# Hybrid decoder layer on one core: the stacked MLP operand as one contiguous piece, wide matmuls in groups, and a rewritten opening unit

## The chip, the core and the metric

The kernel runs on one core of a Trainium2 chip. A core has five engines with queues of their own: TensorE (PE: matmuls and transposes; PEld is its weight load), VectorE (DVE), ScalarE (ACT), GpSimd (POOL) and SyncE (SP, which here only issues transfers). They work in parallel and meet at semaphores. Matmuls write PSUM, which has eight banks of 128 partitions x 512 fp32 values; ACT and DVE read it and write SBUF. The metric is device microseconds of one execution, lower is better.

## The reference, cut to what matters

One decoder layer, 256 positions, width 2048, all fp32. `h = RMSNorm(x)` goes through a wide projection into a gated DeltaNet branch (A), an HGRN2 branch (B), a cross-attention into 256 memory tokens (C) and gates; the branches are merged, projected and added to `x`; then an MLP of width 8192 follows. The two pieces that the change touches are the memory's keys and values, and the MLP:

```
mem_n = rmsnorm(mem, g_mem)                   # (256, 2048)
kv = mem_n @ w_kv                             # (2048 -> 2048): k | v
...
x  = x + rmsnorm(merged @ w_out, g_post_mix)
h2 = rmsnorm(x, g_pre_mlp)
m  = square(relu(h2 @ w_mlp_in)) @ w_mlp_out  # 2048 -> 8192 -> 2048
x  = x + rmsnorm(m, g_post_mlp)
```

## The kernel before, in words

**Precision.** Every large product is formed from split operands: `hi` is the value rounded to the matmul type fp32r, `lo` is the rest. `a @ w` is `hi*hi + hi*lo + lo*hi`, three matmuls into one PSUM accumulation. Weights arrive as fp32 tiles `w` of 2 k-tiles x 512 columns (512 KB, one transfer on SP's queue, four buffers). ACT casts them to `wh` (L145), and DVE subtracts to get `wl` (L147).

**Units.** A unit is 512 output columns over all k-tiles. Kind "x" (L182 to L184) holds 128 positions stationary and streams 512 weight columns; kind "w" (L189 to L191) holds 128 weight columns stationary and streams 256 positions. In both, three matmuls follow each other per product. The third form is `unit_stacked` (L207, L208), used for 15 of the 16 units of the MLP's first matrix. Stationary are 128 weight columns; a first, wide matmul streams `hi` and `lo` of the activations together (2 x 256 columns) against `wh`, then a narrow one streams `hi` (256 columns) against `wl`. The four 128-column blocks `c` of a weight tile go to four banks. The activations stand in tiles `h2h` made by `h8`, laid out `[hi/lo, k-tile, 256]`, so that `hi` and `lo` of one k-tile lie four k-tiles apart and the wide matmul's moving operand has two pieces.

**The MLP.** It runs in eight steps of 1024 hidden columns: `mlp_in(e)` is two units (32 k-tile visits, 128 wide-narrow pairs), then `mlp_out(e-1)` is four kind "x" units of 8 k-tiles (192 matmuls). `mlp_in` evicts each of the four banks with an ACT copy and a DVE add (L1112 and the line after).

**The opening.** Nothing can be multiplied before memory, gain and weights are there. Unit 0 (values of the memory, kind "x") fetches `mem` in `load_mem` between its weight loads, turns it on TensorE (`tr`, L232), and evicts the transposes with the gain as a column scale: `split_scaled` has ACT write `memh` (L216) and DVE write `meml` (L217), k-tile by k-tile. Two k-tiles share one PSUM bank. The program's framework does not let two engines touch a bank at once: the ACT eviction of the second k-tile waits for the DVE eviction of the first. The order of instructions on each engine is chosen by a scheduler, except those that are pinned in program order (`keep_in_program_order`, here `pin`). The squares of `mem` (L325) for the norm run after unit 0, as the first step of `gen_start`, a generator whose steps are pumped one per weight group; it also loads `x` and the small vectors.

**The turn from mixer to MLP.** `mix_last(ps, t)` finishes the residual for 128 positions: a square, a reciprocal root on POOL, four updates of `x` on DVE, and for each of four column chunks `c` four transposes into one bank and four `split_scaled` calls into `h2h`.

Of the kernel before, what the change touches and what calls it, by code (L numbers as in the profile page):

```python
# [33 lines left out]
KG = 2  # L34
BL = 16
WB = 4
NPIN = 1
# [4 lines left out]
def tile_trunk(ctx: ExitStack, tc, a):  # L42
# [23 lines left out]
    def h8(name):  # L66

        return hp.tile([P, 2, 4, S], F32R, tag="h", name=nm(name))
# [24 lines left out]
    pinned = [NPIN]  # L93
# [6 lines left out]
    def load_gcol(names, c0, q):  # L100
        n = len(names) * 16
        grow = const(f"grow{c0}", [n, P])
        for i, x_ in enumerate(names):
            q(grow[i * 16:(i + 1) * 16, :], a[x_][0].rearrange("(c p) -> c p", p=P))
        pg = bank("gcol")
        T.transpose(pg[:, 0:n], grow, ident[0:n, 0:n])
        V.tensor_copy(gcol[:, c0:c0 + n], pg[:, 0:n])

    load_gcol(["g_mem"], 0, adma)
# [28 lines left out]
    def load_w(src, k0, n, c0, width=512, home=None):  # L138
        w = wp.tile([P, KG, 512], F32, tag="w", name=nm("w"), bufs=WB)
        nc.sync.dma_start(  # L140
            w[:, 0:n, 0:width],
            src[k0 * P:(k0 + n) * P, c0:c0 + width].rearrange("(k p) n -> p k n", p=P),
        )
        wh = home("wh") if home else wp.tile([P, KG, 512], F32R, tag="wh", name=nm("wh"))
        i_hi = A.copy(wh[:, 0:n, 0:width], w[:, 0:n, 0:width])  # L145
        wl = home("wl") if home else wp.tile([P, KG, 512], F32R, tag="wl", name=nm("wl"))
        i_lo = V.tensor_tensor(out=wl[:, 0:n, 0:width], in0=w[:, 0:n, 0:width],  # L147
                               in1=wh.bitcast(F32)[:, 0:n, 0:width], op=ALU.subtract)
        if pinned[0] > 0:
            pinned[0] -= 1  # L150
            pin(i_hi)
            pin(i_lo)
        return wh, wl

    def unit(kind, act, nk, src, c0, r0=0, pre=None, order=None, split=False, post=None, ws=None):
# [12 lines left out]
        for i, (g, tt) in enumerate(order):  # L168
            k0 = g * KG
            if pre is not None:  # L170
                pre(k0)
# [25 lines left out]
    def unit_stacked(pairs, nk, src, c0, ps):  # L197


        for g in range(nk // KG):  # L200
            k0 = g * KG
            wh, wl = load_w(src, k0, KG, c0)
            for j in range(KG):
                kt = k0 + j
                both = pairs[kt // 4][:, :, kt % 4, :]
                for c in range(4):
                    T.matmul(ps[c], wh[:, j, c * P:(c + 1) * P], both, start=kt == 0, stop=False)  # L207
                    T.matmul(ps[c][:, 0:S], wl[:, j, c * P:(c + 1) * P], both[:, 0, :], start=False, stop=kt == nk - 1)  # L208
# [5 lines left out]
    def split_scaled(ps, hi, lo, col):  # L214

        A.activation(hi, ps, AF.Copy, scale=col)  # L216
        V.scalar_tensor_tensor(out=lo, in0=ps, scalar=col, in1=hi.bitcast(F32),  # L217
                               op0=ALU.mult, op1=ALU.subtract)
# [5 lines left out]
    def transpose_chunk(src, tiles, c, col0, halves=(0, 1)):  # L224

        hi, lo = tiles
        for half in halves:
# [6 lines left out]
            for q in range(2):  # L234
                kk = half * 2 + q
# [21 lines left out]
    def load_mem(k0):  # L257
# [6 lines left out]
        for sl in cols:  # L264
            nc.sync.dma_start(t[:, :, sl], mem_r[:, :, c * 512 + sl.start:c * 512 + sl.stop])
# [921 lines left out]
```

## Time and profile before

| | |
|---|---|
| median of 3 runs (lowest to highest) | 1843.23 us (1843.05 to 1844.44) |
| profiled execution, its own time | 1843.67 us |
| span of its instructions | 1841.9 us, so 1.8 us lie around it |
| PE busy in the span | 1819.5 us (99%) |
| DVE, ACT busy | 1111.0 us (60%), 900.3 us (49%) |
| first slice of 46 us: PE busy | 7 tenths |

A matmul's busy time in this profile is modelled and runs into the next one: a 512-column matmul reads 0.39 us, while the next starts 0.227 us later. What one really costs is read from the distance between starts, or from the number of matmuls in a stretch. A view by windows lists for each stretch the busy time of each engine with its number of instructions in brackets, then the granted TensorE clock, the mean busy share of the DMA engines and GB/s.

### The profile page before, as it was taken

To read this page: it belongs to the slowest core of one execution; us is meant where nothing else is said; L and a number is where in the kernel's file an instruction comes from. 1 tells how busy PE (TensorE), PEld (TensorE's weight loads), DVE (VectorE), ACT (ScalarE), POOL (GpSimd) and SP (SyncE) were. 2 spreads that over 40 slices of the span, in tenths; PEclk is the share of its full clock that TensorE was granted. 3 is DMA by queue.
4 is the path that set the end of the run, shared out by engine and by line. 5 is a ranking of instruction groups with operands and counts; after the bars stand their busy time and mean duration, and the time that the engine had idled before them with its cause. 6 is when DMAs were issued, how large, how long until landed. Compare 5 with 4: busy or idle time off the path is not lost.

```text
span 1841.9 us, 25658 instructions
## 1 busy us (share of the span) xinstructions
PE 1819.5 (99%) x10214; PEld 1586.4 (86%) x10214; DVE 1111.0 (60%) x1414; ACT 900.3 (49%) x1126; POOL 39.9 (2%) x68
## 2 busy tenths in 40 slices
PE   7999999999999999999999999999999999999997
PEld 5999999988899898888888888888888888888886
DVE  4755576764763685875455557655556565656556
ACT  5644565544545565644444445544444444444443
POOL 1000000200100000000000000000000000000000
PEclk9999999999999999999999999999999999999999
DMA  6766556664584555555766675666666666666663
GB/s 207 234 173 181 152 149 177 176 187 125 169 211 133 153 170 150 158 163 171 217 185 188 196 231 170 186 193 191 189 192 188 190 215 186 194 185 194 186 192 136
DMA packets 174649, 333.52 MB, mean 181 GB/s; under 512 B 13096, under 2 KB 14272, under 8 KB 174272
## 3 DMA queue, kind: packets, MB, share of 16 engines
q1 hardware_dynamic: 168976, 325.10, 58.6%
q10 hardware_dynamic: 4528, 4.54, 0.9%
q0 software_dynamic: 1024, 2.23, 0.7%
q8 instruction: 80, 1.31, 0.3%
q14 instruction: 41, 0.34, 0.1%
HBM read 329.60 MB, written 2.23 MB: 180 GB/s over the span
## 4 chain that ended last, share of the span: by engine, by line
PE 97%; DVE 1%; DMA 0%; issue 0%; ACT 0%; SPq 0%; POOL 0%; DVEq 0%; POOLq 0%; ACTq 0%
PE mm L182 18%; PE mm L184 18%; PE mm L183 18%; PE mm L207 12%; PE mm L208 6%; PE mm L189 6%; PE mm L191 6%; PE mm L190 6%; PE pa L917 1%; PE pw L745 1%; PE pzt L750 1%; DMA mem<-in_mem 0%; DVE wl L147 0%; PE tr L232 0%; PE ab L532 0%
## 5 line engine op out<-in xcount | busy, mean ns | idle before, releaser
L147 DVE TENSOR_TENSOR wl<-w,wh 128x1024 fp32r<-128x1024 f32 x608 | 741.1, 1223 | 596.8 <-ACT wh L145 595.6
L145 ACT CAST wh<-w 128x1024 fp32r<-128x1024 f32 x608 | 637.3, 1051 | 809.8 <-PE mm L184 470.4
L207 PE MATMUL mm<-h2h,wh 128*128 128x512 f32 x960 | 338.6, 398 | 0.0
L208 PE MATMUL mm<-h2h,wl 128*128 128x256 f32 x960 | 269.0, 280 | 0.0
L182 PE MATMUL mm<-wh,hh 128*128 128x512 f32 x576 | 228.4, 397 | 0.0
L184 PE MATMUL mm<-wh,hh 128*128 128x512 f32 x576 | 224.9, 391 | 0.0
L183 PE MATMUL mm<-wl,hh 128*128 128x512 f32 x576 | 224.3, 389 | 0.0
L189 PE MATMUL mm<-hh,wh 128*128 128x256 f32 x768 | 218.8, 285 | 0.0
L207 PEld LDWEIGHTS mm<-h2h,wh 128*128 128x128 f32 x960 | 180.3, 188 | 44.3
L191 PE MATMUL mm<-hh,wl 128*128 128x256 f32 x768 | 217.4, 283 | 0.1
L190 PE MATMUL mm<-hh,wh 128*128 128x256 f32 x768 | 217.3, 283 | 0.0
L182 PE MATMUL mm<-wh,mh 128*128 128x512 f32 x512 | 199.4, 389 | 0.0
L184 PE MATMUL mm<-wh,ml 128*128 128x512 f32 x512 | 199.3, 389 | 0.0
L183 PE MATMUL mm<-wl,mh 128*128 128x512 f32 x512 | 199.2, 389 | 0.0
L208 PEld LDWEIGHTS mm<-h2h,wl 128*128 128x128 f32 x960 | 181.2, 189 | 0.3
L189 PEld LDWEIGHTS mm<-hh,wh 128*128 128x128 f32 x768 | 147.3, 192 | 0.2
L191 PEld LDWEIGHTS mm<-hh,wl 128*128 128x128 f32 x768 | 147.2, 192 | 0.3 <-DVE wl L147 0.3
L190 PEld LDWEIGHTS mm<-hh,wh 128*128 128x128 f32 x768 | 147.3, 192 | 0.2
L184 PEld LDWEIGHTS mm<-wh,hh 128*128 128x128 f32 x576 | 108.1, 188 | 23.1
L183 PEld LDWEIGHTS mm<-wl,hh 128*128 128x128 f32 x576 | 108.4, 188 | 20.9
L182 PEld LDWEIGHTS mm<-wh,hh 128*128 128x128 f32 x576 | 108.3, 188 | 20.6
L184 PEld LDWEIGHTS mm<-wh,ml 128*128 128x128 f32 x512 | 96.1, 188 | 20.2
(361 smaller groups left out, 2167.0 us busy)
## 6 DMA issues: line engine op xcount, KB each, us to landing
w<-in_w_in SPq DMA_DIRECT2D x240, 512.0 KB, 3.7
w<-in_w_mlp_in SPq DMA_DIRECT2D x128, 512.0 KB, 3.7
w<-in_w_mlp_out SPq DMA_DIRECT2D x128, 512.0 KB, 3.7
w<-in_w_kv_mem SPq DMA_DIRECT2D x32, 512.0 KB, 5.3
w<-in_w_out SPq DMA_DIRECT2D x32, 512.0 KB, 4.3
w<-in_w_br_c SPq DMA_DIRECT2D x16, 512.0 KB, 4.2
w<-in_w_br_a SPq DMA_DIRECT2D x16, 512.0 KB, 3.9
w<-in_w_br_b SPq DMA_DIRECT2D x16, 512.0 KB, 3.7
```

The source lines that it names most:

```text
L145: i_hi = A.copy(wh[:, 0:n, 0:width], w[:, 0:n, 0:width])
L147: i_lo = V.tensor_tensor(out=wl[:, 0:n, 0:width], in0=w[:, 0:n, 0:width], in1=wh.bitcast(F32)[:, 0:n, 0:width], op=ALU.subtract)
L182: T.matmul(o, st, wh[:, j, :], start=kt == 0, stop=False)
L183: T.matmul(o, st, wl[:, j, :], start=False, stop=False)
L184: T.matmul(o, sl, wh[:, j, :], start=False, stop=kt == nk - 1)
L189: T.matmul(o, sh, ah, start=kt == 0 and c % 2 == 0, stop=False)
L190: T.matmul(o, sh, al, start=False, stop=False)
L191: T.matmul(o, sl, ah, start=False, stop=kt == nk - 1 and c % 2 == 1)
L207: T.matmul(ps[c], wh[:, j, c * P:(c + 1) * P], both, start=kt == 0, stop=False)
L208: T.matmul(ps[c][:, 0:S], wl[:, j, c * P:(c + 1) * P], both[:, 0, :], start=False, stop=kt == nk - 1)
L745: T.matmul(pw[:, b * 64:(b + 1) * 64], U[:, b, :], half_view(X, s, False)[:, b], start=True, stop=True)
L750: T.matmul(pzt[:, b * 64:(b + 1) * 64], W[:, b, :], half_view(XT, s, True)[:, b], start=True, stop=True)
```

## The change

The tiles of `h8` become `[k-tile, hi/lo, 256]`, so `hi` and `lo` of a k-tile are adjacent and the wide matmul's moving operand is one run of 512 columns. `unit_stacked` issues the four wide matmuls of a k-tile, then the four narrow ones. `split_scaled` takes a list and emits all ACT evictions, then all DVE ones. Unit 0 gets a function of its own, `first_unit`: its loads are pinned on SP, its transposes and products on PE, and the evictions and casts of the first two groups on ACT and DVE; the first weight tile comes in two pieces; each k-tile's transposes have a bank of their own; 19 transposes of the identity whose result nobody reads are added around the first real ones; `mem` squares are taken between groups; and `gen_start` issues its small loads at other steps.

```
 def h8(name):
-    return hp.tile([P, 2, 4, S], F32R, tag="h", name=nm(name))
+    return hp.tile([P, 4, 2, S], F32R, tag="h", name=nm(name))
...
 def unit_stacked(pairs, nk, src, c0, ps):
...
-    both = pairs[kt // 4][:, :, kt % 4, :]
+    both = pairs[kt // 4][:, kt % 4].rearrange("p s n -> p (s n)")
     for c in range(4):
         T.matmul(ps[c], wh[:, j, c * P:(c + 1) * P], both, start=kt == 0, stop=False)
-        T.matmul(ps[c][:, 0:S], wl[:, j, c * P:(c + 1) * P], both[:, 0, :], start=False, stop=kt == nk - 1)
+    for c in range(4):
+        T.matmul(ps[c][:, 0:S], wl[:, j, c * P:(c + 1) * P], both[:, 0:S], start=False, stop=kt == nk - 1)
...
-def split_scaled(ps, hi, lo, col):
-    A.activation(hi, ps, AF.Copy, scale=col)
-    V.scalar_tensor_tensor(out=lo, in0=ps, scalar=col, in1=hi.bitcast(F32),
-                           op0=ALU.mult, op1=ALU.subtract)
+def split_scaled(parts, q=lambda i: i):
+    for ps, hi, lo, col in parts:
+        q(A.activation(hi, ps, AF.Copy, scale=col))
+    for ps, hi, lo, col in parts:
+        q(V.scalar_tensor_tensor(out=lo, in0=ps, scalar=col, in1=hi.bitcast(F32),
+                                 op0=ALU.mult, op1=ALU.subtract))
...
+def load_mem(g):
+    c, half = g // 2, g % 2
...
+    if c < 2:
+        sl = slice(half * 256, half * 256 + 256)
+    elif half == 0:
+        sl = slice(0, 512)
+    else:
+        return
+    pin(nc.sync.dma_start(mem_s[c][:, :, sl], mem_r[:, :, c * 512 + sl.start:c * 512 + sl.stop]))
+
+def idle_turns(n):
+    pd = bank("idle")
+    for i in range(n):
+        pin(T.transpose(pd[:, i % 4 * P:(i % 4 + 1) * P], ident, ident))
+
+def first_unit(src, c0):
...
+    def fetch(g):
+        load_mem(g)
+        ws[g] = load_w_raw(src, g * KG, KG, c0, step=1 if g == 0 else None, q=pin)
+    def turn(g):
+        hi, lo = memT[g // 2]
+        parts = []
+        for kt in (g * KG, g * KG + 1):
+            pt, kk = bank("tr"), kt % 4
+            for t in range(NT):
+                pin(T.transpose(pt[:, t * P:(t + 1) * P], mem_s[g // 2][:, t, kk * P:(kk + 1) * P], ident))
+            parts.append((pt[:, 0:S], hi[:, kk, :], lo[:, kk, :], gcol[:, kt:kt + 1]))
+        split_scaled(parts, pin if g < 2 else lambda i: i)
...
+    fetch(0)
+    idle_turns(11)
+    turn_grow(grow_mem, 16, 0, pin)
+    turn(0)
+    idle_turns(8)
+    for g in range(ng):
+        wh, wl = split_w(ws.pop(g), KG, step=1 if g == 0 else None, q=pin if g < 2 else lambda i: i)
+        if g + 1 < ng:
+            fetch(g + 1)
+        products(g * KG, wh, wl)
+        if g + 1 < ng:
+            turn(g + 1)
+        products(g * KG + 1, wh, wl)
+        if g % 2 == 0 and g > 0:
+            sumsq_chunk(mem_s[g // 2 - 1], ssm, g // 2 - 1)
+        tick()
+    sumsq_chunk(mem_s[3], ssm, 3)
...
-            for k in range(4):
-                split_scaled(pt[:, k * P:(k + 1) * P], h2T[c][0][:, k, t * P:(t + 1) * P],
-                             h2T[c][1][:, k, t * P:(t + 1) * P], gcol[:, 32 + c * 4 + k:33 + c * 4 + k])
+            split_scaled([(pt[:, k * P:(k + 1) * P], h2T[c][0][:, k, t * P:(t + 1) * P],
+                           h2T[c][1][:, k, t * P:(t + 1) * P], gcol[:, 32 + c * 4 + k:33 + c * 4 + k]) for k in range(4)])
```

**The order on ACT in the opening.** Each row is an instruction in the order of the engine: line, operation, what is written from what, shape. `memh` from `tr` is the eviction of one k-tile of the turned memory, `wh` from `w` a weight cast (each number is another tile), `junk` a square of `mem`. Before, from the first eviction on:

```order
L216 ACTIVATE memh_128<-tr_131,gcol 128x256
L216 ACTIVATE memh_128<-tr_159,gcol 128x256
L216 ACTIVATE memh_128<-tr_131,gcol 128x256
L145 CAST wh_142<-w_140 128x1024
L216 ACTIVATE memh_128<-tr_159,gcol 128x256
L145 CAST wh_170<-w_168 128x1024
L145 CAST wh_201<-w_199 128x1024
L145 CAST wh_228<-w_226 128x1024
L145 CAST wh_259<-w_257 128x1024
L145 CAST wh_286<-w_284 128x1024
L216 ACTIVATE memh_187<-tr_190,gcol 128x256
L216 ACTIVATE memh_187<-tr_217,gcol 128x256
```

And with the change:

```order
L222 ACTIVATE memh_126<-tr_147,gcol 128x256
L222 ACTIVATE memh_126<-tr_150,gcol 128x256
L153 CAST wh_166<-w_129 128x512 x2
L222 ACTIVATE memh_126<-tr_181,gcol 128x256
L222 ACTIVATE memh_126<-tr_184,gcol 128x256
L153 CAST wh_197<-w_173 128x1024
L153 CAST wh_229<-w_205 128x1024
L153 CAST wh_262<-w_234 128x1024
L222 ACTIVATE memh_202<-tr_213,gcol 128x256
L222 ACTIVATE memh_202<-tr_216,gcol 128x256
L389 ACTIVATE junk_258,ssm<-mem_125 128x512
```

The first cast stood behind evictions of k-tiles of both halves of the first memory chunk; it is now two half casts behind the first two k-tiles. The casts of weight tiles 1, 2 and 3 stand ahead of the eviction of the fifth k-tile, and squares come between. Four groups on, the cast of weight tile 4 stands behind the evictions of k-tiles 8 and 9:

```order
L222 ACTIVATE memh_267<-tr_278,gcol 128x256
L222 ACTIVATE memh_267<-tr_281,gcol 128x256
L153 CAST wh_294<-w_270 128x1024
L389 ACTIVATE junk_322,ssm<-mem_201 128x512
L389 ACTIVATE junk_324,ssm<-mem_201 128x512
L153 CAST wh_326<-w_298 128x1024
```

Here the tile `memh_267` holds k-tiles 8 to 11, and `wh_326` is weight tile 5.

**The order on PE in the MLP.** The first k-tile of the first stacked unit, before (the four `mm` tiles are the four banks):

```order
L207 MATMUL mm_10326<-h2h_9893,wh_10332 128x512
L208 MATMUL mm_10326<-h2h_9893,wl_10334 128x256
L207 MATMUL mm_10327<-h2h_9893,wh_10332 128x512
L208 MATMUL mm_10327<-h2h_9893,wl_10334 128x256
L207 MATMUL mm_10328<-h2h_9893,wh_10332 128x512
L208 MATMUL mm_10328<-h2h_9893,wl_10334 128x256
```

And with the change:

```order
L211 MATMUL mm_10359<-h2h_9926,wh_10365 128x512
L211 MATMUL mm_10360<-h2h_9926,wh_10365 128x512
L211 MATMUL mm_10361<-h2h_9926,wh_10365 128x512
L211 MATMUL mm_10362<-h2h_9926,wh_10365 128x512
L213 MATMUL mm_10359<-h2h_9926,wl_10366 128x256
L213 MATMUL mm_10360<-h2h_9926,wl_10366 128x256
```

Wide and narrow alternated bank by bank; now four wide ones are followed by four narrow ones.

**The order on ACT at the turn to the MLP.** In `mix_last` for the first 128 positions, each `tr` tile is the bank of one column chunk with four transposes, and `junk` from `mm` is the square of the other 128 positions. Before:

```order
L216 ACTIVATE h2h_9893<-tr_10056,gcol 128x128
L216 ACTIVATE h2h_9894<-tr_10070,gcol 128x128
L216 ACTIVATE h2h_9895<-tr_10085,gcol 128x128
L216 ACTIVATE h2h_9893<-tr_10056,gcol 128x128
L999 ACTIVATE junk_10118,sty<-mm_9898 128x512
L216 ACTIVATE h2h_9894<-tr_10070,gcol 128x128
L216 ACTIVATE h2h_9893<-tr_10056,gcol 128x128
```

And with the change:

```order
L222 ACTIVATE h2h_9926<-tr_10089,gcol 128x128 x4
L222 ACTIVATE h2h_9927<-tr_10103,gcol 128x128 x4
L222 ACTIVATE h2h_9928<-tr_10118,gcol 128x128 x4
L1059 ACTIVATE junk_10151,sty<-mm_9931 128x512
L222 ACTIVATE h2h_9929<-tr_10132,gcol 128x128 x4
```

The four evictions of a bank stood apart, with those of other banks and DVE's between them; they now follow each other.

132 lines of the change are left out of this document (67 added, 65 removed).

## The prediction, made before the result was known

> **What bounds the kernel now.** I read the page's busy times and slices first, then the chain of waits, then the first 60 us by windows and in order of time.
>
> ```profile
> PE 1819.5 (99%) x10214; PEld 1586.4 (86%) x10214; DVE 1111.0 (60%) x1414; ACT 900.3 (49%) x1126; POOL 39.9 (2%) x68
> PE   7999999999999999999999999999999999999997
> PE 97%; DVE 1%; DMA 0%; issue 0%; ACT 0%; SPq 0%; POOL 0%; DVEq 0%; POOLq 0%; ACTq 0%
> PE mm L182 18%; PE mm L184 18%; PE mm L183 18%; PE mm L207 12%; PE mm L208 6%; PE mm L189 6%; PE mm L191 6%; PE mm L190 6%; PE pa L917 1%; PE pw L745 1%; PE pzt L750 1%; DMA mem<-in_mem 0%; DVE wl L147 0%; PE tr L232 0%; PE ab L532 0%
> ```
>
> TensorE bounds everything: 99% of the span, 97% of the chain. Its only slice under 9 tenths inside the run is the first. So there are two ways to a gain: fewer nanoseconds per matmul, or less waiting in the opening. For the second I count. The first view lists wide-matmul instructions up to 67 us; the other row is the first matmul of the unit after the two "x" units.
>
> ```profile
> 0.00:67.00 67.00, 48.76 (x193) 1.00 0.67 223
> 66.94 0.28 PE L189 MATMUL mm<-memh,wh 128*128 128x256 f32 x1
> 36.86 1.04 PE L232 MATMUL tr<-ident,mem 128*128 128x128 f32 x8
> ...
> 37.66 0.48 PE L182 MATMUL mm<-wh,memh 128*128 128x512 f32 x1
> ```
>
> Two units are 192 wide matmuls, and the 193rd row is the one at 66.94. At 0.227 us they are 43.6 us; 32 transposes at 0.11 (eight lie between 36.86 and 37.66) are 3.5, seven small ones about 1.0: 48.1 us of work. The opening therefore loses 66.94 - 48.1 = 18.8 us, 4.5 of them before the first transpose. After it I found no wait of PE over 0.3 us.
>
> **Part 1, the wide-narrow pairs.** The row of a matmul overlaps the next one, so I take starts. These are the first and the next unit's first matmul of one MLP step, then of the step after.
>
> ```profile
> 1256.04 0.39 PE L207 MATMUL mm<-h2h,wh 128*128 128x512 f32 x1
> 1301.25 0.40 PE L182 MATMUL mm<-wh,mh 128*128 128x512 f32 x1
> 1344.83 0.39 PE L207 MATMUL mm<-h2h,wh 128*128 128x512 f32 x1
> 1165.00:1208.00 43.00, 43.00 (x126) 23.26 (x125) 1.00 0.60 186
> 1346.00:1389.00 43.00, 43.00 (x123) 22.87 (x122) 1.00 0.62 188
> 67.30 0.28 PE L189 MATMUL mm<-memh,wh 128*128 128x256 f32 x1
> ...
> 73.90 0.28 PE L190 MATMUL mm<-meml,wh 128*128 128x256 f32 x1
> ```
>
> 128 pairs take 1301.25 - 1256.04 = 45.21 us, 353.2 ns each. 192 contiguous wide ones take 43.58, 227.0 each. Fifty-five narrow ones of kind "w" take 73.90 - 67.30 = 6.60, 120.0 each. A pair at those two prices is 347.0 ns: 6.2 is excess. But the excess is not always there. In 43 us one stretch of the same code (1165 to 1208, inside the first three stacked units) holds 126 wide ones where a later one holds 123: about 346 ns against 353. So two pieces do not cost by themselves at every phase, and I can't say from this trace whether the pieces or the alternation let the stream fall into the slow phase. The change removes both. Six steps like the quoted one, 768 pairs x 6.2 = 4.8 us, and some 45 slow pairs (0.3) ahead of 1165 make 5.1. Bounds: 0 if the grouped stream meets a like phase, -6.0 if all 960 were slow. I take **-5.0**, since the price of unmixed streams has thousands of instances. Grouping delays the eviction of the first bank by three pairs less three narrow ones (0.7 us) per unit; the following unit uses other banks, and L1112 has a whole unit (22 us) to finish. If that cover were gone it would cost 15 x 0.7 = 10 us.
>
> **Part 2, the opening.** These rows carry it.
>
> ```profile
> 1.30 0.29 POOL L85 TENSOR_SCALAR_AFFINE_SELECT ident<-ident 128x128 f32<-128x128 f32 x1
> 4.46 1.12 PE L232 MATMUL tr<-ident,mem 128*128 128x128 f32 x4 [0.15 <-DMA mem<-in_mem]
> 7.69 1.12 PE L232 MATMUL tr<-ident,mem 128*128 128x128 f32 x4 [2.11 <-DMA mem<-in_mem]
> 9.57 1.04 ACT L145 CAST wh<-w 128x1024 fp32r<-128x1024 f32 x1
> 10.67 0.79 PE L182 MATMUL mm<-wh,memh 128*128 128x512 f32 x1 [1.86 <-ACT wh L145]
> 13.03 0.69 PE L232 MATMUL tr<-ident,mem 128*128 128x128 f32 x2 [1.57 <-DMA mem<-in_mem]
> 16.93 0.63 PE L182 MATMUL mm<-wh,memh 128*128 128x512 f32 x1
> 17.66 0.39 PE L184 MATMUL mm<-wh,meml 128*128 128x512 f32 x1
> 17.89 0.40 PE L182 MATMUL mm<-wh,memh 128*128 128x512 f32 x1
> 23.59 0.87 ACT L216 ACTIVATE memh<-tr,gcol 128x256 fp32r<-128x256 f32 x2 [0.95 <-DVE meml L217]
> 23.61 0.51 PE L184 MATMUL mm<-wh,meml 128*128 128x512 f32 x1 [0.55 <-DVE meml L217]
> L145 ACT CAST wh<-w 128x1024 fp32r<-128x1024 f32 x15 | 15.4, 1049 | 13.9 <-PE mm L184 12.9 <-PE pc L361 0.9
> L216 ACT ACTIVATE memh<-tr,gcol 128x256 fp32r<-128x256 f32 x16 | 6.9, 472 | 7.7 <-PE tr L232 5.6 <-DVE meml L217 2.1
> L325 ACT ACTIVATE junk<-mem 128x512 f32<-128x512 f32 x8 | 4.9, 622 | 0.0
> L147 DVE TENSOR_TENSOR wl<-w,wh 128x1024 fp32r<-128x1024 f32 x15 | 18.2, 1222 | 13.9 <-ACT wh L145 13.9
> L217 DVE SCALAR_TENSOR_TENSOR meml<-tr,gcol,memh 128x256 fp32r<-128x256 f32 x16 | 7.1, 479 | 4.8 <-ACT memh L216 4.7
> ```
>
> Before, the first cast (9.57) stands behind evictions that need the second memory piece (7.69), so products start at 10.67, stop for that piece's like at 13.03, and run slowly (0.42 us apart) until 17.4. At 23.59 ACT waits 0.95 for DVE on a shared bank, and PE 0.55 behind it.
>
> With the change the first transposes stay at 4.46, as their transfer is still first. Two pairs at 0.22 and two evictions (0.84 for two before) give 5.8; the first half cast (half of 1.05) 6.35: the first product starts at 6.4, 4.3 earlier. From there I walk the new order with 12 x 0.227 + 4 x 0.11 = 3.2 us of PE per group, ACT 1.05 a cast and 0.42 an eviction, 0.81 a square with its read, DVE 1.23 a split and 0.46 an eviction, and 0.06 per hand-over. PE then waits: 0.5 for the first split (half of 1.22); in group 1 for cast and split behind the evictions of the second piece, 0.6 + 1.1; in group 2, whose evictions stand behind the cast of weight tile 3, 0.1 + 0.9. That tile has 3 MB up to its end, as many as had landed at 13.03 before, with two more small pieces; I take 13.4. In group 4 the cast stands behind the evictions of group 3's middle: 0.6 + 1.1. In group 7, 0.3 behind squares; at unit 1, 0.2 + 1.1 behind the last square and four small loads. That is 6.5 after the start. With 6.4 less 0.44 of transposes before it: 12.5 us lost instead of 18.8, a gain of 6.3. Banks of their own are inside this (no wait as at 23.59). Squares (8 x 0.81) and small loads move on ACT, not on PE; ACT idles 12.9 us behind PE in the first 60, so they lie in cover, but for the waits counted. SP issues the memory pieces ahead of weights; from weight tile 4 on it waits for DVE's splits, and memory piece 3 stands behind tile 5: each still lands 3 us or more before its use by my walk.
>
> My walk has no slack in some 25 hand-overs; at 0.10 instead of 0.06 they are 1.0 more: **-5.4**. Bounds: +0.1, if group 4's wait of 1.7 comes in each of seven groups (11.9 instead of 6.5); and -7.9, if the hand-overs cost nothing more and the waits behind squares and loads (0.3 + 1.3) fall away.
>
> The clock: before, ten products run 0.42 us apart instead of 0.23 (the last at 16.93), 2.0 us that the 18.8 include. The added transposes need only the identity (L85 ends at 1.59), so PE works from 1.7 on, and my walk has every product at full rate. No row shows a transpose alone ending the slow phase: before, the bursts at 4.46 and 7.69 had gaps after them, and it took 13.03 to 17.4 of dense work. If the products alone count, some twelve are slow: 2.4 us, of which the waits in groups 1 and 2 hide about 0.6. [...]
>
> **Part 3, the turn to the MLP.**
>
> ```profile
> 1119.11 0.40 PE L182 MATMUL mm<-wh,h2h 128*128 128x512 f32 x1
> 1122.40 0.50 PE L182 MATMUL mm<-wh,h2h 128*128 128x512 f32 x1 [0.27 <-ACT h2h L216]
> 1128.90 0.74 DVE L1017 SCALAR_TENSOR_TENSOR x<-y,ry,x 128x512 f32<-128x512 f32 x1
> 1133.96 0.39 PE L182 MATMUL mm<-wh,h2h 128*128 128x512 f32 x1
> ```
>
> From 1119.11 to the first product of the third chunk at 1133.96 lie 48 wide matmuls (10.9) and 20 transposes (2.2): 13.1 us of work in 14.85, 1.75 lost, 0.27 at 1122.40 for an ACT eviction that had to alternate with DVE's. Bank by bank the evictions run without alternation, and the last update of x (1128.90) comes before DVE's second sixteen evictions instead of among them, at about 1127.3. But the fourth bank comes free only after the first bank's four DVE evictions. I count 0.6 lost on PE, with 0.3 for hand-overs: **-0.8**, bounds -1.3 and +0.6 (DVE's next weight split, which now stands behind all sixteen, late by one eviction bank).
>
> Tail and middle: their order on the engines is the same but for copies that change places with casts; nothing counted.
>
> **Sum.** -5.0 - 5.4 - 0.8 = -11.2 from the profiled 1843.67, whose span is 1841.9 with 1.8 around it, gives 1832.5. That execution lies 0.4 above the median, within the spread of the runs; I leave it at 1832.5.
>
> **Rivals.**
> First, the pair stays at 353 because the slow phase comes from the stream's start and not from pieces or order: 1837.5. For it: both prices occur in the same code. Against: unmixed streams hold 227 and 120 everywhere. 0.14.
> Second, the opening's waits recur in every group, so that 5.4 us are not gained: 1837.9. For it: casts stand behind evictions and squares on ACT, in order. Against: two groups take 6.3 us on PE and 5.4 on ACT (2 x 1.05 + 4 x 0.42 + 2 x 0.81), so ACT catches up. 0.10.
> Third, the clock stays slow through the first twelve products: +1.8 net: 1834.3. 0.20.
> Fourth, on the other side, weight loads bind.
>
> ```profile
> L208 PEld LDWEIGHTS mm<-h2h,wl 128*128 128x128 f32 x960 | 181.2, 189 | 0.3
> L191 PEld LDWEIGHTS mm<-hh,wl 128*128 128x128 f32 x768 | 147.2, 192 | 0.3 <-DVE wl L147 0.3
> ```
>
> A load takes 189 ns. Alternating, each narrow one's load has a wide matmul beside it; grouped, three of four narrow loads have only a narrow one. If that bound, three of four narrow gaps would go from 120 to 189: 3 x 0.069 x 240 k-tiles = 50 us, so 1882; it decides from a narrow gap of 0.136 on (0.0156 x 720 = 11.2 us, all that is gained). Against: L191's loads take 192 and their matmuls follow each other at 120, and before, each wide one's load already had only a narrow matmul beside it. [...] Chance 0.03.
> Fifth, first and second together, the change does not do what it says: 1843. 0.03.
>
> **How the numbers follow.** The forecast has 0.50, so predicted is 1832.5, its own range 1829 to 1836. Below lies the open walk (-7.9) with -6.0 and -1.3: 1828.5. Above, rivals one and two at 1838 belong inside, with a microsecond for their spread: 1828 to 1839.5. About 0.2%, 3.7 us, can be told from no change here: faster than 1839.5 are forecast and rivals one to three but for their edges, 0.88; same 0.08 (rival five and edges); slower 0.04.
>
> **What would show it.** Starts of the first product near 6.4 and of the unit after the "x" units near 61.5; 45.2 us of an MLP step's 128 pairs down to 44.4; a PE wait of about 1.7 at the fifth weight tile; product starts 0.227 apart from the first on, or 0.42 if the clock waits. A narrow gap above 0.12, or waits on casts in every group, would make it wrong.

## The result, and the profile after

| | before | after |
|---|---|---|
| median of 4 runs each on one chip (lowest to highest) | 1843.14 us (1842.77 to 1844.44) | 1833.40 us (1832.87 to 1833.79) |
| ratio | | 0.9946, 95% interval 0.9928 to 0.9963 |
| span of the profiled execution | 1841.9 us | 1831.6 us |

The change is worth 9.7 us, 0.54%. The prediction was 1832.5. The page of the changed kernel: busy time of TensorE, its slices, and the chain of waits by engine.

```profile
PE 1818.7 (99%) x10233; PEld 1589.3 (87%) x10233; DVE 1110.5 (61%) x1415; ACT 897.6 (49%) x1127; POOL 39.9 (2%) x68
PE   9999999999999999999999999999999999999998
PE 98%; DVE 1%; ACT 1%; DMA 0%; issue 0%; SPq 0%; ACTq 0%; DVEq 0%; POOLq 0%; POOL 0%
```

The first slice has gone from 7 tenths to 9. TensorE still bounds everything; the rest of the change lies inside its stream and is seen only in starts. First the opening, in order of time on PE (start, busy time, engine, line, what is written from what, and in square brackets the idle time before it and its releaser).

```profile
1.64 2.61 PE L280 MATMUL idle<-ident 128*128 128x128 f32 x11 [1.64 <-POOL ident L84]
4.54 1.11 PE L298 MATMUL tr<-ident,mem 128*128 128x128 f32 x4
5.45 1.92 PE L280 MATMUL idle<-ident 128*128 128x128 f32 x8
7.01 0.78 PE L308 MATMUL mm<-wh,memh 128*128 128x512 f32 x1
8.29 0.40 PE L308 MATMUL mm<-wh,memh 128*128 128x512 f32 x1
...
11.22 0.50 PE L308 MATMUL mm<-wh,memh 128*128 128x512 f32 x1 [0.25 <-ACT wh L153]
12.48 0.50 PE L309 MATMUL mm<-wl,memh 128*128 128x512 f32 x1 [0.76 <-DVE wl L154]
...
22.76 0.50 PE L308 MATMUL mm<-wh,memh 128*128 128x512 f32 x1 [0.25 <-ACT wh L153]
24.02 0.50 PE L309 MATMUL mm<-wl,memh 128*128 128x512 f32 x1 [0.76 <-DVE wl L154]
...
36.68 0.50 PE L187 MATMUL mm<-wl,memh 128*128 128x512 f32 x1
...
59.81 0.28 PE L193 MATMUL mm<-memh,wh 128*128 128x256 f32 x1
```

The first product stands at 7.01 instead of 10.67, and from the third on they follow each other at full rate. PE still waits at two of the eight weight tiles, the second (11.22, 12.48) and the fifth (22.76, 24.02). The bracket gives less than PE loses: 24.02 - 22.76 is 1.26 for a matmul of 0.23, so 1.03 are lost, and 0.42 ahead of it. The unit after the two "x" units starts at 59.81 instead of 66.94.

Next the starts of the first stacked part (three units) and of the unit behind it, the same for one MLP step, and the turn: the last four updates of `x` and the first product of the third chunk, of which the prediction gave the times before.

```profile
1136.65 0.62 PE L211 MATMUL mm<-h2h,wh 128*128 128x512 f32 x2
1204.83 0.40 PE L186 MATMUL mm<-wh,mh 128*128 128x512 f32 x1
1248.38 0.61 PE L211 MATMUL mm<-h2h,wh 128*128 128x512 f32 x2
1293.26 0.40 PE L186 MATMUL mm<-wh,mh 128*128 128x512 f32 x1
...
1112.10 0.40 PE L186 MATMUL mm<-wh,h2h 128*128 128x512 f32 x1
1117.38 2.74 DVE L1077 SCALAR_TENSOR_TENSOR x<-y,ry,x 128x512 f32<-128x512 f32 x4
1125.77 0.39 PE L186 MATMUL mm<-wh,h2h 128*128 128x512 f32 x1
```

The same two ends of the first stacked part in the kernel before:

```profile
1144.84 0.39 PE L207 MATMUL mm<-h2h,wh 128*128 128x512 f32 x1
1212.49 0.39 PE L182 MATMUL mm<-wh,mh 128*128 128x512 f32 x1
```

From these starts the whole difference can be put together (all in us):

| stretch | before | after | difference |
|---|---|---|---|
| to the unit after the "x" units | 66.94 | 59.81 | -7.13 |
| from there to the first stacked product | 1077.90 | 1076.84 | -1.06 |
| first stacked part, three units | 67.65 | 68.18 | +0.53 |
| six MLP steps, 128 pairs each | 6 x 45.21 | 6 x 44.88 | -1.98 |
| from the last of them to the end of the span | 96.7 | 96.1 | -0.6 |

That is -10.2 of the -10.3 between the spans; the units between the steps are the same to 0.01 us each. The last row's 0.6 lies behind the last matmul, where the output is written; nothing of the change runs there.

So the time came out nearly as predicted, but not the parts: the opening gave more than was forecast, the stacked stream far less. The experiments go to these two.

### The profile page after: what moved, and what is told of

It is laid out like the page before. It is cut to its first block, busy times and chain, and to the rows that moved or that the text cites. A ratio compares the mean times of both kernels' runs of the same rounds, so it can differ in the third digit from the quotient of the medians.

```text
span 1831.6 us, 25712 instructions
## 1 busy us (share of the span) xinstructions
PE 1818.7 (99%) x10233; PEld 1589.3 (87%) x10233; DVE 1110.5 (61%) x1415; ACT 897.6 (49%) x1127; POOL 39.9 (2%) x68
## 4 chain that ended last, share of the span: by engine, by line
PE 98%; DVE 1%; ACT 1%; DMA 0%; issue 0%; SPq 0%; ACTq 0%; DVEq 0%; POOLq 0%; POOL 0%
PE mm L186 18%; PE mm L188 18%; PE mm L187 18%; PE mm L211 12%; PE mm L213 6%; PE mm L193 6%; PE mm L195 6%; PE mm L194 6%; PE pa L977 1%; PE pw L805 1%; PE pzt L810 1%; DMA w<-in_w_kv_mem 0%; DVE wl L154 0%; ACT wh L153 0%; PE tr L1081 0%
## 5 line engine op out<-in xcount | busy, mean ns | idle before, releaser
L154 DVE TENSOR_TENSOR wl<-w,wh 128x1024 fp32r<-128x1024 f32 (+1 forms) x609 | 741.6, 1221 | 589.5 <-ACT wh L153 588.0
L153 ACT CAST wh<-w 128x1024 fp32r<-128x1024 f32 (+1 forms) x609 | 638.0, 1050 | 806.6 <-PE mm L188 452.8
L211 PE MATMUL mm<-h2h,wh 128*128 128x512 f32 x960 | 262.0, 394 | 0.0
L211 PEld LDWEIGHTS mm<-h2h,wh 128*128 128x128 f32 x960 | 164.5, 189 | 22.4
L213 PEld LDWEIGHTS mm<-h2h,wl 128*128 128x128 f32 x960 | 147.3, 189 | 20.4
L213 PE MATMUL mm<-h2h,wl 128*128 128x256 f32 x960 | 152.7, 281 | 0.0
L188 PEld LDWEIGHTS mm<-wh,ml 128*128 128x128 f32 x512 | 96.1, 188 | 20.0
```

What stands on the lines that cost most here:

```text
L153: q(A.copy(wh[:, js, 0:width], w[:, js, 0:width]))
L154: q(V.tensor_tensor(out=wl[:, js, 0:width], in0=w[:, js, 0:width], in1=wh.bitcast(F32)[:, js, 0:width], op=ALU.subtract))
L188: T.matmul(o, sl, wh[:, j, :], start=False, stop=kt == nk - 1)
```

## Experiment 1: pieces, or the order of wide and narrow?

Three kernels, all with the changed opening and turn. In `unit_stacked` the body became a list of (wide or narrow, k-tile, column block), chosen by MLP step, so that one run shows six orders (shortened). All six steps are alike in the kernel before and in the changed one, so the lengths of steps can be compared with each other.

```
+ORDERS = {2: "alt", 3: "altg", 4: "rev", 5: "two", 6: "eight", 7: "serp"}
...
-            for j in range(KG):
-                for c in range(4): T.matmul(ps[c], wh..., both, ...)
-                for c in range(4): T.matmul(ps[c][:, 0:S], wl..., both[:, 0:S], ...)
+            for o, j, c in seq(k0):      # the step's order over the two k-tiles
+                if o == "W": T.matmul(ps[c], wh[:, j, ...], both(j), ...)
+                else:        T.matmul(ps[c][:, 0:S], wl[:, j, ...], hi(j), ...)
```

The second kernel has the same with `h8` in two pieces, the third two pieces and "alt" in all steps.

> The changed kernel, with another order of the stacked products in each of the last six MLP steps; the operand stays one piece. W is a wide product, N a narrow one. Steps in turn: W N alternating; alternating but for the first k-tile of each unit, which stays four and four; alternating with N first from the second k-tile on; W W N N; eight W and eight N (two k-tiles together); W4 N4 N4 W4. In the changed kernel each of these steps takes 44.88 us for 128 pairs, in the kernel before 45.21, and at 227 and 120 ns it would be 44.42. Theory 1 (the change between widths costs, some 14 ns each time the stream goes from wide to narrow and back): eight and eight and W4 N4 N4 W4 come near 44.65, W W N N near 45.3, alternating at 46.2. Theory 2 (a rhythm that the stream locks into when it starts, as the kernel before shows 346.7 ns and 353 ns per pair in one and the same code): alternating is 44.4 or 45.2, and the variants of its start differ by just that. Theory 3 (the two pieces cost): alternating in one piece is near 44.4 in all three alternating steps.

> The changed kernel with the stacked operand in two pieces again, as before, and in the last six MLP steps another order each: W N alternating (as in the kernel before); four and four (as in the changed one); alternating after a first k-tile of four and four; alternating with N first; W W N N; eight and eight. Theory 3 (pieces cost): every order is 0.3 us or more above the same order in one piece, four and four near 45.2. Theories 1 and 2 (pieces cost nothing): every order as in one piece, to 0.05 us: alternating 45.21, four and four 44.88.

> The changed kernel with the stacked products as before (two pieces, W N alternating, in all MLP steps): the opening and the turn alone. The two traces give the stacked part 1.45 us of the gain (six steps of 0.33, less 0.53 lost in the first), so 1834.9 if that holds; 1838.4 if the stacked part was worth the 5.0 us of the prediction. The six last steps should go back to 45.21 each.

Measured lengths of a step in us, W a wide and N a narrow product (from the first stacked product to the first product of the unit behind):

| order | one piece | two pieces |
|---|---|---|
| W N alternating | 45.21 | 45.21 |
| four and four | 44.88 | 44.88 |
| alternating, first k-tile of each unit four and four | 44.79 | 44.79 |
| alternating, N first from the second k-tile on | 44.79 | 44.79 |
| W W N N | 44.58 | 44.58 |
| eight and eight | 44.67 | 44.67 |
| W4 N4 N4 W4 | 44.69 | not run |

A figure below the second row is one step of one execution; the two kernels took 1832.12 and 1832.57 us. The pieces cost nothing in the six orders that both have (theory 3 falls), so one half of the change's edit here does nothing. Theory 1 falls too: W W N N changes width twice as often as four and four and is faster. What is left is the rhythm of theory 2. It shows inside the third row's step of the one-piece kernel. Two stretches of 15 us, one in each unit of the step, by windows: time, PE busy with its number of matmuls, and so on.

```profile
1340.00:1355.00 15.00, 15.00 (x87) 13.03 (x86) 6.43 (x6) 5.77 (x6) 0.00 (x0) 1.00 0.69 185
1365.00:1380.00 15.00, 15.00 (x89) 13.26 (x88) 8.47 (x8) 7.24 (x7) 0.00 (x0) 1.00 0.57 179
```

87 matmuls in the first, 89 in the second: from one start to another over 16 pairs, the first unit runs at 353 ns per pair, and from the first k-tile of the second unit on at 346.7. One and the same alternating stream has two steady rates. The old stack's run shows how loosely that hangs on the program: its first stacked part took 68.70 us, where the kernel before, with the same order of matmuls, took 67.65, because there the stream had gone over to 346.7 behind the second of the two bursts of four transposes in that part, and here it had not. Its steps are back at 45.21, and its time is 1836.07 us, 2.7 above the changed kernel; 6 x 0.33 for the steps and 0.52 for the first part are 2.5 of that. The expected 1834.9 had taken the first part's 67.65 for a property of the order.

## Experiment 2: one disturbance

> The changed kernel, one piece, with W N alternating in the last six MLP steps but for a disturbance in the first unit of each step. In turn: second k-tile as W4 N4 in both units of the step; second k-tile as W4 N4 in the first unit only; N first from the second k-tile on in the first unit, W first again in the second unit; second, third and fourth k-tiles as W4 N4, first unit only; second k-tile as W W N N W W N N, first unit only; second, fourth and sixth k-tiles as W4 N4, first unit only. Theory A (a running alternating stream at 353 ns per pair goes over to 346.7 as soon as its order is disturbed, and stays there): all six near 44.4 us, against 44.58 for the best order so far. Theory B (the crossing at the middle of the step is what did it, or the disturbance has to meet a certain point of the rhythm of three pairs): some of the six stay at 45.2, or go over at their middle only and take 44.8.

The kernel took 1833.48 us, one execution; its steps:

| disturbance of the alternating stream (one piece) | step, us |
|---|---|
| second k-tile four and four, in both units | 44.80 |
| second k-tile four and four, in the first unit only | 44.40 |
| N first from the second k-tile on, in the first unit only | 45.20 |
| second to fourth k-tile four and four, first unit | 45.20 |
| second k-tile W W N N twice, first unit | 45.19 |
| second, fourth and sixth k-tile four and four, first unit | 44.48 |

Start and end of the second and the fourth:

```profile
1336.94 0.39 PE L252 MATMUL mm<-h2h,wh 128*128 128x512 f32 x1
1381.34 0.39 PE L187 MATMUL mm<-wh,mh 128*128 128x512 f32 x1
...
1513.68 0.39 PE L252 MATMUL mm<-h2h,wh 128*128 128x512 f32 x1
1558.88 0.40 PE L187 MATMUL mm<-wh,mh 128*128 128x512 f32 x1
```

Theory B: the disturbance has to be of a certain kind and in a certain place. One group of four and four turns 353 into 346.7 to the end of the step; a second one in the next unit turns it back (first row: 346.7 in the first unit, 353 in the second); three in a row leave it slow (45.20 us). The same edit was then made in the kernel before, and nothing else:

```
+                cs = [(x, c) for c in range(4) for x in "WN"]
+                if kt == 1 and e >= 2 and c0 // 512 % 2 == 0:
+                    cs = [(x, c) for x in "WN" for c in range(4)]
```

> The kernel before, and one k-tile in each of the last six MLP steps changed: the second one of the first unit as W4 N4, all others alternating, two pieces as they were. If the disturbance and not the layout, nor anything else of the change, sets the rhythm: 44.40 instead of 45.21 in each of the six steps, 4.9 us in all, 1838.3 to 1839; the opening and the turn as before. If the changed kernel's other parts matter for it: 45.2 and 1843 to 1844.

1838.74 us against 1843.99, ratio 0.9971 (0.9959 to 0.9984), as expected. One of its six steps, start and end:

```profile
1256.45 0.39 PE L211 MATMUL mm<-h2h,wh 128*128 128x512 f32 x1
1300.86 0.39 PE L182 MATMUL mm<-wh,mh 128*128 128x512 f32 x1
```

44.41 us, with two pieces and the old opening. Eight matmuls per step in another order save 0.80 us, more than twice what grouping all 256 saved. All six steps agree to 0.01 us, here and in the two later kernels with this edit. (Its first stacked part, not edited, took 68.70, the slow way.) Why the stream has two rates stays open: in the slow one the gaps between starts repeat every three pairs (233, 117, 241, 120, 236, 113 ns), in the fast one every two (231, 112, 233, 117, in the first stacked part of the kernel before) or every one (230, 117, behind the disturbance), and the records of weight loads, which start 2 to 5 ns behind each matmul in both, don't tell what sets them.

## Experiment 3: the transposes that nobody reads

> The changed kernel without the nineteen transposes of the identity at the start; all else the same. Theory A (transposes count for whatever makes the first products slow): without them the first ten products or so run 0.42 us apart instead of 0.23, and the products of the unit after the x units start 1.5 to 2.0 us later than 59.8: near 61.5, and the time is near 1835. Theory B (only products count, or the products' own start was enough): the first products look as in the changed kernel, the unit starts at 59.8, time 1833.4.

1834.34 us, 0.9 above the changed kernel. Products and transposes on PE around the point where the rate changes, and the unit after the "x" units:

```profile
9.35 0.63 PE L310 MATMUL mm<-wh,meml 128*128 128x512 f32 x1
9.78 0.95 PE L298 MATMUL tr<-ident,mem 128*128 128x128 f32 x4
10.48 0.48 PE L308 MATMUL mm<-wh,memh 128*128 128x512 f32 x1
10.79 0.39 PE L309 MATMUL mm<-wl,memh 128*128 128x512 f32 x1
...
60.74 0.28 PE L193 MATMUL mm<-memh,wh 128*128 128x256 f32 x1
```

Six products run at the slow rate (from the third on 0.43 us apart) and four transposes behind them (0.21), up to 10.4; theory A, but with six slow products instead of ten. The unit starts 0.93 later and not 1.5 to 2.0, and that number is not clean: without the pinned transposes the scheduler moved a cast elsewhere, and the waits of the fifth tile (1.45) came back at the seventh as 2.05. So it was done again on a kernel whose ACT and DVE order is fixed by hand (experiment 4's).

> The kernel with the casts ahead, without the nineteen transposes of the identity; ACT and DVE keep their order by hand, so that unlike in the run without them before nothing else moves. In casts_ahead the transposes of the identity go over from 214 to 109 ns at 6.3 us, before the first wide product, and the unit after the x units starts at 55.86. Theory A (transposes alone bring the clock up): the first six or more products are 0.43 us apart, and the unit starts 1.0 to 1.5 us later, 56.9 to 57.4. Theory B (they bring nothing): 55.9 or, without the turns in the first product's way, a little less.

```profile
57.58 0.28 PE L193 MATMUL mm<-memh,wh 128*128 128x256 f32 x1
```

57.58 against 55.85: 1.7 us, somewhat more than expected, and 1831.54 (one execution) against 1829.58 in time. Theory A holds. The sharper evidence is the run of the old stack, whose opening is the changed kernel's. Its second group of eight transposes, ahead of any product:

```profile
5.46 1.26 PE L305 MATMUL idle<-ident 128*128 128x128 f32 x8
6.74 0.50 PE L333 MATMUL mm<-wh,memh 128*128 128x512 f32 x1
```

Eight took 1.92 us in the changed kernel (5.45, above) and 1.26 here: single starts are 0.214 apart up to 5.9 and 0.109 from 6.0 on. Transposes alone had ended the slow phase. Of the ten profiles that have both groups, seven changed their rate so, between 5.4 and 6.9 us, while only transposes had run since 1.64; the other three within their first three products, by 8.3. So with the added transposes the rate changed 3.8 to 6.7 us after the first of them, and in the run without them 3.7 us after its first product (6.75). A view by windows gives a granted clock of 1.00 from the start, in the slow phase and behind it; but that view reads 1.00 where the trace has no record of the clock, and the first record (1.00) begins at 8.05 us in the changed kernel and at 17.52 in the kernel before, where in each the slow products end (at 8.04; between 17.35 and 17.66).

## Experiment 4: the waits of the opening

At the fifth weight tile of the changed kernel, ACT, then DVE:

```profile
20.93 0.84 ACT L222 ACTIVATE memh<-tr,gcol 128x256 fp32r<-128x256 f32 x2 [2.35 <-PE tr L298]
21.66 1.04 ACT L153 CAST wh<-w 128x1024 fp32r<-128x1024 f32 x1
...
22.74 1.23 DVE L154 TENSOR_TENSOR wl<-w,wh 128x1024 fp32r<-128x1024 f32 x1 [0.42 <-ACT wh L153]
```

The cast (21.66) stands behind two evictions that had to wait 2.35 us for transposes; its tile had landed at 16.17. The edit splits the next weight tile ahead of the evictions of its memory piece, spreads the squares over the groups, and pins the whole order (shortened):

```
-            if g + 1 < ng:
-                turn(g + 1)                      # transposes, evictions
+            if g + 1 < ng:
+                parts = turns(g + 1)             # transposes alone
+                nxt = split_w(ws.pop(g + 1), KG, q=pin)
+                split_scaled(parts, pin)         # for g == 0 in halves: cast, eviction, cast, eviction
             products(g * KG + 1, wh, wl)
-            if g % 2 == 0 and g > 0:
-                sumsq_chunk(mem_s[g // 2 - 1], ssm, g // 2 - 1)
+            square(g)                            # one or two squares of mem, pinned
```

> The changed kernel with another order on ACT and DVE in the opening unit: the cast and split of the next weight tile stand ahead of the evictions of its memory piece in every group (for the second tile in halves, each with its eviction), and one or two of the eight squares behind them in each group, in this order on both engines. In the changed kernel PE waits 0.42 and 1.03 us at the second and again at the fifth weight tile, and 0.2 at two places more. Theory 1 (the casts came late because evictions stood ahead of them on ACT): these waits vanish, the unit after the x units starts near 56.6 instead of 59.8, and the time is near 1830.2. Theory 2 (what is late is the weight tile's transfer): the waits stay, now with the evictions late behind the casts too, and the unit starts at 59.8 or later.

1829.58 us, ratio to before 0.9921 (0.9904 to 0.9937). The casts of the second tile on ACT, and the unit after the "x" units on PE:

```profile
9.31 0.62 ACT L336 CAST wh<-w 128x512 fp32r<-128x512 f32 x1 [2.03 <-DMA w<-in_w_kv_mem]
9.84 0.47 ACT L222 ACTIVATE memh<-tr,gcol 128x256 fp32r<-128x256 f32 x1
10.21 0.61 ACT L336 CAST wh<-w 128x512 fp32r<-128x512 f32 x1
...
55.85 0.28 PE L193 MATMUL mm<-memh,wh 128*128 128x256 f32 x1
```

Theory 1, and more than expected: 55.85 instead of 56.6. All waits behind casts are gone; the only one left above 0.12 us is for the first split. The next limit is near: the cast at 9.31 waits 2.03 us for its tile, though PE does not yet lose more than 0.11 us by it.

## Experiment 5: the smaller parts

Two k-tiles in the halves of one bank again, in the opening; and the alternating evictions again, at the turn:

```
-            for kt in (g * KG, g * KG + 1):
-                pt, kk = bank("tr"), kt % 4
+            pt = bank("tr")
+            for q, kt in enumerate((g * KG, g * KG + 1)):    # writes pt[:, q * S + ...]
```

> The changed kernel with the two k-tiles of an opening group in the halves of one bank, as before; the order of the evictions stays. Theory 1 (two engines do not work on one bank at a time, so DVE's evictions stand behind both of ACT's): each group's second eviction is late by 0.4 us, PE waits some 0.2 to 0.5 us in groups where DVE is behind, and the unit after the x units starts at 60.5 to 62. Theory 2 (the eviction order alone removed the old wait, the banks did nothing): 59.3 to 59.8, as in the changed kernel and the three runs with its opening.

One eviction group, ACT and DVE, of this kernel, and then its unit start; behind it the same group of the changed kernel:

```profile
18.33 0.84 ACT L222 ACTIVATE memh<-tr,gcol 128x256 fp32r<-128x256 f32 x2 [1.14 <-PE tr L299]
19.20 0.88 DVE L224 SCALAR_TENSOR_TENSOR meml<-tr,gcol,memh 128x256 fp32r<-128x256 f32 x2 [2.32 <-ACT memh L222]
...
60.63 0.28 PE L193 MATMUL mm<-memh,wh 128*128 128x256 f32 x1
```

```profile
17.74 0.84 ACT L222 ACTIVATE memh<-tr,gcol 128x256 fp32r<-128x256 f32 x2 [1.21 <-PE tr L298]
18.25 0.88 DVE L224 SCALAR_TENSOR_TENSOR meml<-tr,gcol,memh 128x256 fp32r<-128x256 f32 x2 [1.63 <-ACT memh L222]
```

With one bank DVE starts 0.87 us behind ACT, after both of its evictions; with two, 0.51. The unit starts at 60.63, where the six runs with the changed opening lie between 59.33 and 60.10. Theory 1, at the low end of what it gave: 0.5 to 1.3 us, from one execution (1834.11 us). That figure is no clean price: here, too, the scheduler moved a cast, and the fifth tile's wait of 1.45 came back at the seventh as 1.66. What is clean is the eviction group above.

```
-            split_scaled([(pt[...], ...) for k in range(4)])
+            for k in range(4):
+                split_scaled([(pt[...], ...)])
```

> The changed kernel with the evictions at the turn to the MLP as before: ACT and DVE in alternation on one bank, part by part; the transposed chunks of the first stages keep the new order. From the start of the unit after the x units to the first stacked product are 1077.90 us in the kernel before and 1076.83 in the changed one. If the turn's eviction order is worth the difference of 1.07, this kernel has 1077.9; if the gain came from the other places that use the helper, 1076.8.

```profile
60.10 0.28 PE L193 MATMUL mm<-memh,wh 128*128 128x256 f32 x1
1138.11 0.39 PE L211 MATMUL mm<-h2h,wh 128*128 128x512 f32 x1
```

1138.11 - 60.10 = 1078.01 (one execution, 1834.94 us): the turn's eviction order is the whole difference, and the same helper in the earlier transposes brings nothing. In the eleven profiles with the new order at the turn this stretch takes 1076.75 to 1076.87, in the three with the old one 1077.90 to 1078.01.

## Experiment 6: together

> The kernel with the casts ahead (1829.58 us), and besides: the stacked products alternating W N with the second k-tile as W4 N4 in the first unit of each of the last six MLP steps, W W N N in the three stacked units before them; in the opening unit the two products with the high weights ahead of those with the low ones, k-tile by k-tile; six instead of eight transposes of the identity in the second group. If the rhythm after one disturbance is a property of the order alone, the six steps take 44.40 us as in the run of the disturbances (2.9 less in all), the first stacked part 67.7 (0.5 less), and the opening's wait of 0.5 for the first split goes: 1825.7. If the rhythm depends on what came long before, some steps take 45.2: 1827 to 1831.

1827.00 us, ratio 0.9906 (0.9891 to 0.9920). All six steps take 44.40 and the first stacked part 67.79, as expected; the miss of 1.3 is in the opening:

```profile
9.94 0.62 ACT L352 CAST wh<-w 128x512 fp32r<-128x512 f32 x1 [2.25 <-DMA w<-in_w_kv_mem]
10.99 0.50 PE L329 MATMUL mm<-wh,memh 128*128 128x512 f32 x1 [0.77 <-ACT memh L237]
...
56.79 0.28 PE L194 MATMUL mm<-memh,wh 128*128 128x256 f32 x1
```

The second tile landed at 9.92, and PE, which came earlier by the new order of products, waits longer, for an eviction that stands behind that tile's cast. To see whether that order costs something, the last run left it out:

> The kernel with the casts ahead and the stacked orders of the run of all together (one k-tile of W4 N4 in each of the last six steps, W W N N in the three units before them), and nothing else: the opening's products stand in the changed kernel's order, and eight transposes of the identity in the second group. The stacked part is worth 2.9 and 0.4 us, so 1826.3 if it simply adds to the 1829.58 of the casts ahead. The run of all together took 1827.0; if its order of the opening's products cost something, this one is 0.7 below it; if the difference is the arrival of the second weight tile (9.31 us in one run, 9.94 in the other), the two agree to half a microsecond, and the unit after the x units starts between 55.9 and 56.8, by that arrival.

```profile
9.28 0.62 ACT L351 CAST wh<-w 128x512 fp32r<-128x512 f32 x1 [1.44 <-DMA w<-in_w_kv_mem]
55.91 0.28 PE L194 MATMUL mm<-memh,wh 128*128 128x256 f32 x1
```

1826.13 us, ratio 0.9902 (0.9886 to 0.9919), the fastest of all: 18.1 us under the kernel before on its chip and 7.3 under the changed one, which ran on another chip. Its second tile landed at 9.26. Of the 0.88 between the two unit starts 0.66 is the later start of that tile's cast, if PE feels all of it; the rest may be the product order, which asks early for the low memory part that DVE makes last, but that was not separated. Across the runs with this opening's loads the third tile landed between 10.93 and 12.03, so one profile of an opening can't tell half a microsecond.

## Why the prediction came out right, point by point

The time was inside 1828 to 1839.5 and 0.9 from the forecast, but that closeness is in good part luck: the terms were mis-sized in opposite directions. The first gave 3.6 less than forecast; the second gave 1.7 more, the third 0.3, and the tail 0.6 that nobody had counted.

**Part 1, forecast -5.0, measured -1.4** (6 x -0.33, +0.53), nearer to the first rival's 0 than to the forecast. The step that failed is "I take -5.0, since the price of unmixed streams has thousands of instances". The grouped stream is not unmixed: its pair takes 350.8 ns, not 347.0, since from the second group on its wide matmuls stand 224 to 236 ns apart (232 on average, not 227) and its narrow ones 116 to 120 (119). The prediction had seen both rates of the old stream and left open whether pieces or alternation let it fall into the slow one; it then took the price that would follow if one of the two did. Neither does: pieces cost nothing, and alternation runs at 346.7 after one disturbance. The +0.53 is the reverse side: the stretch of the old kernel that ran fast was lost. It is not a fixed price either, since the same stretch took 68.70 in the run of the kernel before with one disturbance, whose first part was not edited; against that this part would be worth -2.5. The bounds 0 and -6.0 held.

**Part 2, forecast -5.4, measured -7.1**, between the forecast and the bound of -7.9. The walk was right in kind (casts and splits that stand behind evictions) and at the second and fifth tile also in place; at two other places where it had waits there are hardly any. Its sizes:

| | walk | measured |
|---|---|---|
| first product | 6.4 | 7.0 |
| wait for the first split | 0.5 | 0.6 |
| second tile | 1.7 | 1.45 |
| third group's low evictions | 1.0 | 0.24 |
| fifth tile | 1.7 | 1.45 |
| last group and next unit | 1.6 | 0.2 |

The first product was late by 0.6. Part of it is that the eight transposes behind the first real ones ran at the slow rate and stood in its way (5.45 for 1.92 us); without them it is at 6.75. The rest is on ACT, whose first eviction starts at 5.26 and whose half cast takes 0.61 us up to 6.67. The measured 0.6 for the first split holds some 0.2 of the slow rate, which in this run lasted into the second product. The third group's evictions stand behind the cast of the fourth weight tile, which landed nearly as walked (13.51, against 13.4, with 3 MB issued up to its end, as walked); but PE reached the group's products at 15.59, 0.6 later than in the walk, and so waited less. The next unit's cast stood at 34.32, two microseconds ahead of use, since ACT had caught up; the walk carried its lateness too far. So the first product came 0.6 later than walked and the waits behind it are 2.6 shorter; the gaps that are no wait of this table come to 1.4 us, where the forecast had added 1.0 for its hand-overs.

**Part 3, forecast -0.8, measured -1.06** by its stage, and experiment 5 puts all of it on the eviction order. From the first product of the turn to that of the third chunk it takes 13.67 us (1125.77 - 1112.10) instead of 14.85. The updates of `x` came ahead of DVE's second sixteen evictions, as forecast (1117.38, the evictions from 1120.06 on).

**Tail and middle**, forecast nothing: the middle is the same to 0.01 per unit, the tail 0.6 shorter, unexplained and within what one profile can say of its last transfers.

**The rivals.** The first (pair stays at 353 because of the stream's start) came close for the old order, whose rate hangs on what precedes it; the new order has a third rate. The second (waits in every group) fell: two groups of seven. The third (clock slow through twelve products) fell: transposes alone bring the rate up, here within the second product; leaving them out costs 1.7 us. The fourth (weight loads bind) fell: narrow gaps of 116 to 120 ns in groups of four, under loads of 189. The fifth fell.

## What to carry to other kernels

Price a mixed instruction stream only by the same mix: 227 and 120 ns each held in thousands of unmixed instances and did not add up in the mix (347.0 ns a pair by them, 350.8 measured in groups of four), and a single k-tile in another order changed the rate of all that followed in its step (from 353 to 346.7 ns a pair). Where an engine with a strict order holds both a cast whose data is there and evictions that still wait for TensorE (as ACT at 20.93 us in experiment 4), put the cast first: with the squares pinned behind, that was worth 3.8 us on top of the change. A sum that fits is no proof of its terms; read each stage's length before believing it.

## What the hardware showed that was not expected

- A stream of matmuls with moving sizes 512 and 256 has several steady rates, two of them in the same order of instructions: 353.3 or 346.7 ns per alternating pair, 350.8 in groups of four, 349.0 in groups of eight (44.67 us over 128 pairs), 348.3 in W W N N. Which of the two an alternating stream takes is set by what precedes it (one k-tile in another order), and it lasts to the end of a step of 128 pairs (44.40 us for a step instead of 45.21); why is open.
- A moving operand in two runs of 256 costs the same as one run of 512, in six orders (44.88 us a step in groups of four and 45.21 alternating, both ways).
- Transposes alone (of an fp32 identity, with four of the memory among them) bring TensorE from the slow rate (0.214 us each, 0.427 a 512-column matmul) to the full one (0.109 and 0.227), 3.8 to 6.7 us after they begin, those counted that ended in the first products.
